# Down projections of two feed-forward layers: 16 of the 22 hidden chunks by seven-product (Strassen) blocks in two phases

## The chip, the cores and the metric

The kernel runs on one core of a Trainium2 chip. The metric is the device time of one execution in microseconds, the median over several runs. Beside it stands one execution recorded by the hardware profiler, from which all durations are taken.

## The reference

A residual stream h of 1024 positions by 1024 features passes through two layers; each adds a mixer and then a gated feed-forward network, with an RMS norm in front of each, and a last norm ends the program. The change touches only the feed-forward network:

```python
def conv_glu_ffn(x, w_up, conv_w, conv_b, w_down):
    h = causal_depthwise_conv(x @ w_up, conv_w, conv_b)
    gate, val = jnp.split(h, 2, axis=-1)
    return (jax.nn.silu(gate) * val) @ w_down
...
h = h + conv_glu_ffn(rmsnorm(h, ffn_norm[layer]), ffn_up[layer], ffn_conv_w[layer],
                     ffn_conv_b[layer], ffn_down[layer])
```

The hidden width is 2816, which is 22 chunks of 128; gate and value each have 22 chunks. Everything is float32.

## The kernel before

Activations lie transposed, features on the 128 partitions and the 1024 tokens along the row. TensorE multiplies in fp32r, which keeps fewer bits, so every operand is split into a high part (a cast on ScalarE, line 338) and a low part (the difference, on VectorE, line 339), and each product is three matmuls: high x high, high x low, low x high. A matmul has a 128 x 128 weight block and 512 tokens, half of a row. `Weights` (lines 72 to 140) streams weight blocks in the order of a plan: a load on the SP queue into one of two raw buffers `wst` (three while `W.more` is set), then the split (line 116) into a ring of `wh`/`wl` pairs.

The feed-forward network `ffn(ly, norms)` has two stages.

*Up.* For each chunk f of 22, gate and value come from one block of seven products of 12 matmuls each instead of eight (lines 772 to 818, matmuls in line 637): the weights and the tokens are first combined by additions. Beside the products of chunk f run the convolution, silu and product of chunk f-1 (class `Tail`): two activations for the last tap (lines 653, 654), four taps on VectorE (659), silu on ScalarE (667), the product (673), and a store of the 128 x 1024 result to DRAM, tensor `hid` (674). The operands of the up stage lie in AH and AL (8 slots of 1024 tokens) and TH and TL (three sets of 4 x 512).

*Down.* The hidden chunks come back from DRAM, `stage(f, slot)` (lines 731 to 734): a load into a `t4` buffer (four of them) and a split into a slot of AH/AL or TH/TL. They are taken in groups of 8, 6 and 8 chunks in layer 0 and 8, 6, 4 and 4 in layer 1. For each group, each of the 8 output chunks oc and each token half, `down` (831) accumulates all chunks of the group in one of four PSUM banks (839), and VectorE adds the bank to the residual hT (841), which was loaded from DRAM, `hdr`, at the start of the stage (828, 829). The buffers of the up stage and hT share memory, so that load waits until the last chunk's result is stored. In layer 0 the last group runs one token half after the other, with its weights fetched once for each half, and the next norm is woven into it (952 to 964); while that goes on, the pool engine makes the low parts of the next weights (961). In layer 1 the last four chunks are multiplied the other way round, tokens as weights, and end in the output (`finish`).

A scheduler of the compiler lays out the instructions of each engine, by the order of the program and by when it reckons an instruction ready; each engine then works its list in order, and so does the SP queue, which issues nearly all transfers.

Of the kernel before, what the change touches and what calls it, by code (L numbers as in the profile page):

```python
# [37 lines left out]
GROUPS = {0: [(0, 8), (8, 6), (14, 8)], 1: [(0, 8), (8, 6), (14, 4), (18, 4)]}  # L38
# [33 lines left out]
class Weights:  # L72
# [3 lines left out]
    def __init__(self, nc, pool, plan):  # L76
        self.nc, self.pool, self.plan = nc, pool, plan
        self.eng = nc.vector
        self.more = None
        self.raw, self.ready = [], {}  # L80
        self.n_dma = self.n_conv = self.n_get = self.n_take = 0
        self.n_ring = 0

    def _dma(self, n=None):
        n = n or NWST + (self.more is not None)
        while self.n_dma < min(self.n_conv + n, len(self.plan)):
# [10 lines left out]
    def pair(self):  # L97
# [3 lines left out]
        if self.more is not None and n % 5 > 2:  # L101
            return [self.more.tile([P, DC, P], F32R, tag=t, bufs=2, name=f"{t}x{n}")
                    for t in ("wh2", "wl2")]
# [40 lines left out]
def trunk(ctx: ExitStack, tc: tile.TileContext, x, mix0_norm, mix0_w_in, lru_conv_w, lru_conv_b,  # L144
# [12 lines left out]
    plan = []  # L157
# [8 lines left out]
    def plan_ffn(ly):  # L166
# [6 lines left out]
        def dn(h, f0, n):  # L173
            for oc in range(DC):
                plan.append((f"{ly}d{h}{f0}{oc}",
# [3 lines left out]
        for f0, n in GROUPS[ly]:  # L179
# [6 lines left out]
            else:  # L186
                dn("0", f0, n)
                dn("1", f0, n)
# [91 lines left out]

    def open_h(name):
        st["pool"] = tc.tile_pool(name=f"h_{name}", bufs=1, side="right")
        p = st["pool"].__enter__()
        st["hT"] = p.tile([P, DC, T], F32, name=f"hT_{name}")

    def close_h():
        st["pool"].__exit__(None, None, None)
        st["hT"] = None
# [284 lines left out]
    hid = [dram.tile([P, NF, T], F32, name=f"hid{i}") for i in range(2)]  # L573

    def ffn(ly, norms):

# [16 lines left out]
        w2 = [None]  # L593

# [47 lines left out]
        def t4x(name):  # L642
            return w2[0].tile([P, T], F32, tag="t4x", bufs=2, name=name)


        class Tail:
            def __init__(self, f, g, v):
                self.f, self.g, self.v = f, g, v

            def ident(self):  # L650
                f, new = self.f, t4x if w2[0] is not None else t4
                self.cg, self.cv = new(f"cg{ly}{f}"), new(f"cv{ly}{f}")
# [19 lines left out]
            def end(self):  # L672
                dve.tensor_tensor(self.cv, self.cv, self.cg, op=ALU.mult)
                nc.sync.dma_start(hid[ly][:, self.f], self.cv)
# [8 lines left out]
            def whole(self):  # L683
                self.ident()
                self.rest()

# [19 lines left out]
        def tokens(p1):  # L706
# [14 lines left out]
            w2_cm = tc.tile_pool(name=f"w2{ly}", bufs=1)  # L721
            W.more = w2[0] = w2_cm.__enter__()
# [8 lines left out]
        def stage(f, slot):  # L731
            r = t4(f"hr{ly}{f}")
            nc.sync.dma_start(r, hid[ly][:, f])
            split(*slots[slot], r)

# [35 lines left out]

        for f in range(2, NF):
            w, nxt = ws.pop(f), f + 1 if f + 1 < NF else None
# [27 lines left out]
            act.copy(u3, X)  # L801
# [3 lines left out]
            else:  # L805
                for c in range(4):
                    stage(c, c)
# [3 lines left out]
            if nxt:  # L811
                prep_b(nxt)
            prod(X, w["c"], 4, "4", False)
# [5 lines left out]
        W.ahead(2)  # L819
        for c in range(4, 8):  # L820
            stage(c, c)
        prev.rest()
        W.more = w2[0] = None
        w2_cm.__exit__(None, None, None)
# [3 lines left out]
        for c in range(DC):  # L828
            nc.sync.dma_start(hT[:, c], hdr[:, c])

        def down(h, tag, f0, a, oc):
            wh, wl = W.get(f"{ly}d{tag}{f0}{oc}")
# [10 lines left out]
        def finish(f0, a):  # L843
# [81 lines left out]
            for tt in range(DC - 1):  # L925
# [5 lines left out]
                if tt + 2 < DC:  # L931
# [5 lines left out]

        plans = {0: (slots[0:8], [(8 + i, 8 + i) for i in range(6)]),
                 8: (slots[8:14], [(14 + i, i) for i in range(8)]),
                 14: (slots[0:8] if ly == 0 else slots[0:4], []),  # L940
                 18: (slots[4:8], [])}
        for f0, n in GROUPS[ly]:
            a, todo = plans[f0]
            if f0 + n < NF:
                for oc in range(DC):
                    down(None, "x", f0, a, oc)
                    for f, c in todo[oc:oc + 1]:
                        stage(f, c)
            elif ly:
                finish(f0, a)  # L950
            else:
                new = [Norm(0, gcols[after], f"nf{ly}"), Norm(1, gcols[after], f"nf{ly}")]
                rsqrt_set()
                for h in range(2):
                    for oc in range(DC):
                        down(h, str(h), f0, a, oc)
                        if after.startswith("mix"):
                            nc.sync.dma_start(hdr[:, oc, HALF[h]], hT[:, oc, HALF[h]])
                        if h == 1 and oc == 0:
                            new[0].rstd()  # L960
                            W.eng = pool
# [3 lines left out]
        W.eng = dve  # L965
# [618 lines left out]
```

## Time and profile before

| what | value |
|---|---|
| runs, us | 2176.86 median of 3 (2176.27 to 2177.23) |
| the profiled execution, us | 2175.29 |
| its span, first to last instruction, us | 2173.6 |
| granted TensorE clock, mean | 0.998 |
| first down stage, us from the start | 778 to about 1022, 1056 matmuls in line 839 |
| second down stage, up to the last four chunks | 1916 to about 2115, 864 matmuls in line 839 |
| data moved | 212.19 MB, 98 GB/s on the mean |

The page of a profile gives busy time by engine, the span in 40 slices, the DMA queues, the chain of work that ended last and the costliest groups of instructions. A group names the line, engine, operation and tiles, then busy time, mean length of one and the idle time in front of them with what ended it. Matmuls overlap: the length of one in a group is not the pitch at which they follow each other. Other views give the busy time of the engines in any stretch, the timeline of one engine, and who waited for whom.

### The profile page before, as it was taken

Reading aid. Unit: us, or ns where it says so; the run is one execution under the profiler, and the core shown is the slowest. Engines: PE = TensorE matmul, PEld = TensorE weight load, DVE = VectorE, ACT = ScalarE, POOL = GpSimd, SP = SyncE. Lnnn points to the kernel's source line nnn. Section 1 sums busy time; section 2 is a strip of 40 time slices with the busy share of each in tenths; the row PEclk is TensorE's granted clock in tenths of the full one; section 3 lists DMA queues with packets and bytes.
Section 4 is the critical chain, followed back from the end, with each engine's and each line's share of the span. In section 5 each row is a group of like instructions: output and inputs, shape, how many; then the busy total and the mean of one; then the engine's idle time right before and its main releaser. Section 6 shows DMA issues by size and latency. Waiting matters only on the chain. (4 is left out here: it accounts for less than half of the span.)

```text
span 2173.6 us, 25612 instructions
## 1 busy us (share of the span) xinstructions
PE 2138.9 (98%) x9865; PEld 1757.0 (81%) x9865; DVE 1455.4 (67%) x2075; ACT 1016.3 (47%) x1405; POOL 95.4 (4%) x128
## 2 busy tenths in 40 slices
PE   8999999999999999999999999899999999999998
PEld 7888888788888878887778887788778888888887
DVE  6655657987777763347576667868987777763334
ACT  5433544655555541124556565744655555541113
POOL 0000001000000000004111111010000000000000
PEclk9999999999999999999999999999999999999999
DMA  5111342232222282234221211442232222382112
GB/s 149 53 49 49 112 149 88 87 107 84 73 77 88 92 285 73 84 121 131 73 66 52 74 56 54 159 153 81 88 107 87 84 71 78 97 292 94 56 54 78
DMA packets 263329, 212.19 MB, mean 98 GB/s; under 512 B 8336, under 2 KB 233424, under 8 KB 263208
## 3 DMA queue, kind: packets, MB, share of 16 engines
q1 hardware_dynamic: 262872, 210.08, 31.0%
q8 instruction: 77, 1.26, 0.2%
q0 software_dynamic: 192, 0.30, 0.1%
q14 instruction: 44, 0.36, 0.1%
q10 hardware_dynamic: 144, 0.20, 0.0%
HBM read 165.15 MB, written 43.29 MB: 96 GB/s over the span
## 5 line engine op out<-in xcount | busy, mean ns | idle before, releaser
L116 ACT CAST wh<-wst 128x1024 fp32r<-128x1024 f32 (+2 forms) x134 | 134.1, 1001 | 491.7 <-PE dp L839 274.6
L841 DVE TENSOR_TENSOR hT_f<-dp,hT_f 128x512 f32<-128x512 f32 x96 | 65.9, 690 | 225.2 <-PE dp L839 224.0
L116 DVE TENSOR_TENSOR wl<-wst,wh 128x1024 fp32r<-128x1024 f32 (+2 forms) x127 | 146.8, 1156 | 96.7 <-ACT wh L116 96.7
L839 PE MATMUL dp<-AH,wh 128*128 128x512 f32 x432 | 168.1, 391 | 1.4 <-DVE hT_f L841 1.3
L839 PE MATMUL dp<-AL,wh 128*128 128x512 f32 x432 | 167.9, 389 | 0.3 <-DVE AL L339 0.3
L839 PE MATMUL dp<-AH,wl 128*128 128x512 f32 x432 | 167.9, 389 | 0.0
L637 PE MATMUL X<-TH,wh 128*128 128x512 f32 x312 | 121.9, 391 | 1.9 <-ACT u L757 0.9
L637 PE MATMUL X<-TH,wl 128*128 128x512 f32 x312 | 121.7, 390 | 0.3 <-DVE wl L339 0.3
L637 PE MATMUL X<-TL,wh 128*128 128x512 f32 x312 | 121.4, 389 | 0.0
L659 DVE SCALAR_TENSOR_TENSOR cg<-g,par_c,cg 128x1023 f32<-128x1023 f32 x88 | 112.7, 1280 | 2.0 <-ACT cg L653 1.9
L659 DVE SCALAR_TENSOR_TENSOR cv<-v,par_c,cv 128x1023 f32<-128x1023 f32 x88 | 112.5, 1278 | 1.2 <-ACT cv L654 1.1
L338 ACT CAST wh<-wst 128x1024 fp32r<-128x1024 f32 x78 | 80.6, 1053 | 61.4 <-PE YZ L637 38.3
L339 DVE TENSOR_TENSOR wl<-wst,wh 128x1024 fp32r<-128x1024 f32 x78 | 95.1, 1223 | 6.6 <-ACT wh L338 6.6
L839 PEld LDWEIGHTS dp<-AH,wh 128*128 128x128 f32 x432 | 81.1, 188 | 19.4 <-DVE hT_f L841 1.7
L839 PEld LDWEIGHTS dp<-AL,wh 128*128 128x128 f32 x432 | 81.1, 188 | 17.7 <-DVE AL L339 0.7
L839 PEld LDWEIGHTS dp<-AH,wl 128*128 128x128 f32 x432 | 81.1, 188 | 16.8
L345 PE MATMUL op<-AH,wh 128*128 128x512 f32 x192 | 76.3, 397 | 0.6 <-ACT hT_o L520 0.6
L637 PE MATMUL X<-TH,wh2x 128*128 128x512 f32 x192 | 74.8, 390 | 0.7 <-ACT u L791 0.7
L637 PE MATMUL YZ<-AH,wh 128*128 128x512 f32 x192 | 74.9, 390 | 0.0
L345 PE MATMUL op<-AH,wl 128*128 128x512 f32 x192 | 74.8, 390 | 0.0
L345 PE MATMUL op<-AL,wh 128*128 128x512 f32 x192 | 74.8, 389 | 0.0
L637 PE MATMUL YZ<-AL,wh 128*128 128x512 f32 x192 | 74.7, 389 | 0.0
(487 smaller groups left out, 5854.6 us busy)
## 6 DMA issues: line engine op xcount, KB each, us to landing
wst<-in_ffn_up_dram SPq DMA_DIRECT2D x88, 512.0 KB
hid<-cv SPq DMA_DIRECT2D x44, 512.0 KB
hr<-hid SPq DMA_DIRECT2D x44, 512.0 KB
wst<-in_mix_w_in_dram SPq DMA_DIRECT2D x40, 512.0 KB
wst<-in_ffn_down_dram SPq DMA_DIRECT2D x35, 512.0 KB
wst<-in_mix_w_out_dram SPq DMA_DIRECT2D x32, 512.0 KB
hdr<-hT_o SPq DMA_DIRECT2D x32, 256.0 KB
hT_f<-hdr SPq DMA_DIRECT2D x16, 512.0 KB
```

The costliest lines, as they stand in the source:

```text
L116: did = self.nc.scalar.copy(wh[:, :k, :m], w[:, :k, :m]), self.eng.tensor_tensor(wl[:, :k, :m], w[:, :k, :m], wh[:, :k, :m].bitcast(F32), ...
L338: return (act.copy(h, src), (eng or dve).tensor_tensor(l, src, h.bitcast(F32), op=ALU.subtract))
L339: (eng or dve).tensor_tensor(l, src, h.bitcast(F32), op=ALU.subtract))
L345: last_mm = pe.matmul(ps, a[:, k], b[:, k, s], start=(k == 0 and i == 0), stop=(k == DC - 1 and i == 2))
L637: last = pe.matmul(ps, a[:, k0 + k], b[:, k], start=(first and k == 0 and i == 0), stop=(k == 3 and i == 2), skip_group_check=True)
L659: dve.scalar_tensor_tensor(dst[:, dl:], src[:, :T - dl], taps[j](c), dst[:, dl:], op0=ALU.mult, op1=ALU.add)
L839: pe.matmul(ps, p_[:, k], q_[:, s], start=(k == 0 and i == 0), stop=(k == n - 1 and i == 2))
L841: dve.tensor_tensor(hT[:, oc, s], ps, hT[:, oc, s], op=ALU.add)
```

## The change

Chunks 0 to 15 are multiplied in two groups of eight by blocks of seven products (Winograd's form of Strassen's method). The even and the odd chunks of a group are the two halves of the inner dimension, the two token halves are the columns, and two pairs of output chunks the rows; so a block covers 8 chunks, 4 output chunks and all tokens. A product is 2 output chunks (e = 0, 1) x 4 chunks x 3 matmuls of 512 tokens. The seven products are parted by the operands they read. Form A has "11", "2", "3", "4", whose token operands lie in AH and AL, form B has "1", "21", "22" in TH and TL. One form for one set of four output chunks is a `Quad`; the order is A, A, B, B for the first group, then the same for the second. Running sums stay in PSUM: all products of form A go into the same two banks, and after each one VectorE adds the bank to the part of hT that it completes (56 such additions per layer; the first quad's eight are copies on ScalarE that start hT).

Token sums: the up stage computes them beside its products (`Tail.sums`: one half-size subtraction after an even chunk, three after an odd one) and stores seven operands per pair of chunks in a new DRAM tensor `hids`. `bring` loads half an operand and splits it; the lists `beside` say which of them follow each half product. Weight sums: `Quad.x11`, `s2`, `s3`, `s4` compute them on VectorE; two of them (`s`, `s2`) go to DRAM in form A and come back in form B. `prep(n + 2)` runs two products ahead, and loads for the next quad are issued at fixed steps of it.

Chunks 16 to 21 stay plain: six in layer 0, with weights split once and kept in TH and TL for both token halves; two and then four in layer 1. The pool engine no longer makes low parts of weights at the end of layer 0. hT is two tiles of four output chunks; rows 4 to 7 are loaded from `hdr` at the start of the stage, rows 0 to 3 are added during the second form-A phase (`residual_in`). The ring of weight pairs shrinks from five to four in the up stage, and the buffers of the convolution are one `cg` and two `cv`, by even and odd chunk.

```diff
-GROUPS = {0: [(0, 8), (8, 6), (14, 8)], 1: [(0, 8), (8, 6), (14, 4), (18, 4)]}
+EIGHTS = (0, 8)
+PLAIN = {0: [(16, 6)], 1: [(16, 2), (18, 4)]}
+OPS = {"11": 0, "2": 1, "4": 2, "3": 3, "21": 4, "22": 5, "1": 6}
 HALF = (slice(0, H), slice(H, T))
...
-                dn("1", f0, n)
...
+        for i in (1, 0):
+            cm = tc.tile_pool(name=f"h{i}_{name}", bufs=1, side="right")
+            st["pool"].append(cm)
+            tiles.insert(0, cm.__enter__().tile([P, 4, T], F32, name=f"hT{i}_{name}"))
+        st["hT"] = Halves(tiles)
...
+                self.cg, self.cv = (w2[1].tile([P, T], F32, tag=t, name=f"{t[:2]}{ly}{f}")
+                                    for t in ("cg", f"cv{f % 2}"))
...
+                f, to, k = self.f, hids[ly][self.f // 8 % 2], self.f % 8 // 2
+                if f >= PLAIN[ly][0][0]:
+                    nc.sync.dma_start(hid[ly][:, f], self.cv)
+                elif f % 2:
+                    nc.sync.dma_start(to[:, 4:6, k],
+                                      self.cv.rearrange("p (s t) -> p s t", t=H))
+                else:
+                    nc.sync.dma_start(to[:, OPS["11"], k], self.cv[:, HALF[0]])
+            def sums(self):
+                f, to, k = self.f, hids[ly][self.f // 8 % 2], self.f % 8 // 2
+                if f >= PLAIN[ly][0][0]:
+                    return
+                b1, b2 = (self.cv[:, s] for s in HALF)
+                if f % 2 == 0:
+                    t1 = w2[0].tile([P, H], F32, tag="t1", name=f"t1{ly}{f}")
+                    dve.tensor_tensor(t1, b2, b1, op=ALU.subtract)
+                    nc.sync.dma_start(to[:, OPS["1"], k], t1)
+                    Tail.even = self.cv, t1
+                else:
+                    ev, t1 = Tail.even
+                    Tail.even = None
+                    e1, e2 = (ev[:, s] for s in HALF)
+                    dve.tensor_tensor(t1, b2, t1, op=ALU.subtract)
+                    dve.tensor_tensor(e2, b2, e2, op=ALU.subtract)
+                    dve.tensor_tensor(e1, b1, t1, op=ALU.subtract)
+                    nc.sync.dma_start(to[:, OPS["2"], k], t1)
+                    nc.sync.dma_start(to[:, 2:4, k], ev.rearrange("p (s t) -> p s t", t=H))
...
+        def bring(g, y, j):
+            ks = slice(2 * j, 2 * j + 2)
+            r = t4(f"br{ly}{g}{y}{j}").rearrange("p (k t) -> p k t", k=2)
+            nc.sync.dma_start(r, hids[ly][g][:, OPS[y], ks])
+            split(*(t[:, ks] for t in B[y]), r)
...
+            def load(self, i):
+                def wst(n, src):
+                    t = self.raw[n] = wpool.tile([P, DC, P], F32, tag="wst", bufs=NWST,
+                                                 name=f"{n}{self.name}")
+                    nc.sync.dma_start(t if n == "s1" else two(t), src)
+                def small(n, src):
+                    t = self.raw[n] = [t2(f"{n}{e}{self.name}").rearrange("p (k m) -> p k m", k=4)
+                                       for e in range(2)]
+                    for e in range(2):
+                        nc.sync.dma_start(t[e], src(e))
+                if self.form == "A":
+                    if i == 0:
+                        wst("x11", self.block(0, self.oc, 2))
+                    else:
+                        wst("x21", self.block(0, self.oc + 2, 2))
+                        small("x22", lambda e: self.block(1, self.oc + 2 + e, 1))
+                elif i == 0:
+                    wst("s1", self.sum[0].rearrange("p e k m -> p (e k) m"))
+                else:
+                    wst("x12", self.block(1, self.oc, 2))
+                    small("s2", lambda e: self.sum[1][:, e])
...
+            def x11(self):
+                split(*self.pair("11"), self.raw["x11"])
+                s = self.raw["s"] = [t2(f"s{e}{self.name}").rearrange("p (k m) -> p k m", k=4)
+                                     for e in range(2)]
+                for e in range(2):
+                    dve.tensor_tensor(s[e], one(self.raw["x21"], e), self.raw["x22"][e],
+                                      op=ALU.add)
+                    nc.sync.dma_start(self.sum[0][:, e], s[e])
+            def s2(self):
+                s = self.raw.pop("s")
+                for e in range(2):
+                    dve.tensor_tensor(s[e], s[e], one(self.raw["x11"], e), op=ALU.subtract)
+                    nc.sync.dma_start(self.sum[1][:, e], s[e])
+                self.split2("2", s)
+            def s3(self):
+                t, a = self.raw.pop("x21"), self.raw.pop("x11")
+                dve.tensor_tensor(t, a, t, op=ALU.subtract)
+                split(*self.pair("3"), t)
+            def x22(self):
+                self.split2("4", self.raw.pop("x22"))
+            def s1(self):
+                split(*self.pair("1"), self.raw.pop("s1"))
+            def x12(self):
+                split(*self.pair("21"), self.raw["x12"])
+            def s4(self):
+                t, a = self.raw.pop("s2"), self.raw.pop("x12")
+                for e in range(2):
+                    dve.tensor_tensor(t[e], one(a, e), t[e], op=ALU.subtract)
+                self.split2("22", t)
...
+            def prod(self, n, e):
+                bank = (n == "21", e)
+                first = n in ("11", "1", "21")
+                if first:
+                    self.ps[bank] = psml(f"dq{self.name}{n}{e}")
+                ps = self.ps[bank]
+                (xh, xl), (yh, yl) = self.w[n], B[n]
+                for k in range(4):
+                    for i, (a, b) in enumerate(((xh, yh), (xh, yl), (xl, yh))):
+                        pe.matmul(ps, a[:, 4 * e + k if n == "1" else 2 * k + e], b[:, k],
+                                  start=(first and k == 0 and i == 0),
+                                  stop=(k == 3 and i == 2), skip_group_check=True)
+                row, s = {"11": (0, A0), "2": (0, A1), "3": (1, A1), "4": (1, A0),
+                          "1": (1, A1), "21": (0, A0), "22": (0, A1)}[n]
+                at = st["hT"][:, self.oc + 2 * row + e, s]
+                if self.form == "A" and self.g == 0 and self.oc == 0:
+                    act.copy(at, ps)
+                else:
+                    dve.tensor_tensor(at, ps, at, op=ALU.add)
+                if n in ("4", "21", "22"):
+                    del self.ps[bank]
+                if e:
+                    del self.w[n]
...
+        quads = [Quad(g, oc, form) for g in range(2) for form in "AB" for oc in (0, 4)]
+        steps_ = [(q, i) for q in quads for i in range(len(q.preps))]
+        def prep(n):
+            q, i = steps_[n]
+            q.preps[i]()
+            nxt = quads.index(q) + 1
+            if nxt < len(quads):
+                if q.form == "A":
+                    loads = {2: (0, 1)}.get(i, ())
+                else:
+                    loads = {0: (0,), 2: (1,)}.get(i, ())
+                for j in loads:
+                    quads[nxt].load(j)
...
+        n_kept = PLAIN[0][0][1]
+        kept = [[t.rearrange("p a b t -> p (a b t)").rearrange(
+            "p (o k m) -> p o k m", o=DC, m=P)[:, oc] for t in (TH, TL)] for oc in range(DC)]
+        def kept_in(oc):
+            split(*kept[oc], W.take(f"{ly}d0{PLAIN[0][0][0]}{oc}")[:, :n_kept])
+            W.done()
+        def lead_in(i):
+            if ly == 0:
+                kept_in(i)
+            else:
+                W.ahead(i + 1)
+        def residual_in(c):
+            r = t4(f"hd{ly}{c}")
+            nc.sync.dma_start(r, hdr[:, c])
+            dve.tensor_tensor(hT[:, c], hT[:, c], r, op=ALU.add)
+        beside = {(0, "A"): first_[6:] + brings(0, ("1", "21", "22")),
+                  (0, "B"): brings(1, ("11", "2", "3", "4")),
+                  (1, "A"): [x for c, b in enumerate(brings(1, ("1", "21", "22")))
+                             for x in [b] + ([lambda c=c: residual_in(c)] if c < 4 else [])],
+                  (1, "B"): [lambda i=i: stage(PLAIN[ly][0][0] + i, i) for i in range(6)]}
+        for n, (q, i) in enumerate(steps_):
+            todo = beside[q.g, q.form]
+            for e in range(2):
+                q.prod(q.prods[i], e)
+                if e == 0 and n + 2 < len(steps_):
+                    prep(n + 2)
+                if todo:
+                    todo.pop(0)()
+            if n == len(steps_) - 2:
+                W.limit = None
+                W._dma()
+                lead_in(0)
+            elif n == len(steps_) - 1:
+                lead_in(1)
...
+        for f0, n in PLAIN[ly]:
+            a = slots[f0 - PLAIN[ly][0][0]:][:n]
...
-                        down(h, str(h), f0, a, oc)
+                        if not h and oc + 2 < DC:
+                            kept_in(oc + 2)
+                        down(h, kept[oc], f0, a, oc)
                         if after.startswith("mix"):
                             nc.sync.dma_start(hdr[:, oc, HALF[h]], hT[:, oc, HALF[h]])
                         if h == 1 and oc == 0:
                             new[0].rstd()
-                            W.eng = pool
```

127 lines of the change are left out of this document (89 added, 38 removed).

## The prediction

> **What bounds the kernel now.** I read the page first, then the busy time by stage, the chain of waits, the groups of the two stages that change, and last the waits and the timeline around the change of stage.
>
> ```profile
> span 2173.6 us, 25612 instructions
> ...
> PE 2138.9 (98%) x9865; PEld 1757.0 (81%) x9865; DVE 1455.4 (67%) x2075; ACT 1016.3 (47%) x1405; POOL 95.4 (4%) x128
> ```
>
> Busy time by stage: the up and the down stage of layer 0, then those of layer 1; the columns are start:end, length, then each engine's busy time (instructions), granted clock, DMA share and GB/s.
>
> ```profile
> 389.00:778.00 389.00, 387.94 (x1707) 319.70 (x1706) 311.60 (x339) 209.97 (x253) 0.00 (x0) 1.00 0.31 95
> 778.00:1022.00 244.00, 242.35 (x1064) 199.16 (x1064) 116.01 (x122) 68.47 (x78) 24.49 (x11) 1.00 0.41 134
> 1512.00:1916.00 404.00, 401.68 (x1762) 329.54 (x1761) 325.37 (x351) 221.32 (x264) 0.00 (x0) 1.00 0.30 93
> 1916.00:2115.00 199.00, 198.18 (x877) 163.47 (x876) 81.97 (x96) 42.23 (x46) 0.00 (x0) 1.00 0.35 117
> ```
>
> TensorE is full in both stages. VectorE has 116 of 244 us of work in the first down stage and 82 of 199 in the second, but 80% in the up stages. So matmuls taken out of a down stage shorten it one for one, as long as VectorE, ScalarE and the DMA queues keep up with what replaces them.
>
> The chain of waits gives the pitch of the matmuls (start, length, work):
>
> ```profile
> 1862.58 2.72 PE YZ L637 x12
> ...
> 1925.86 188.45 PE dp L839 x830
> ```
>
> 188.45 / 830 = 0.227 us, and 2.72 / 12 is the same. The groups of the first down stage give one matmul as 391 ns (busy, mean | idle before, releaser):
>
> ```profile
> L839 PE MATMUL dp<-AH,wh 128*128 128x512 f32 x194 | 75.1, 391 | 1.4 <-DVE hT_f L841 1.3
> ```
>
> That is a pipelined length, not a price; I reckon with 0.227.
>
> **The matmuls removed.** Eight chunks, four output chunks and both token halves cost 8 x 4 x 3 x 2 = 192 matmuls now. A pair of quads makes them with 7 products x 2 output chunks x 4 k x 3 = 168. There are two groups of eight and two sets of four output chunks in each layer: 4 x 24 = 96 less per layer, 192 in all, and the page should count 9,865 - 192 = 9,673. 192 x 0.227 = **-43.5 us**. Sixteen chunks still cost 672 matmuls, 152.4 us, in each layer; the plain rest is unchanged in kind.
>
> **VectorE in the new products.** The prices, from the groups of the first down stage and, for an operand of half size, of the second up stage:
>
> ```profile
> L841 DVE TENSOR_TENSOR hT_f<-dp,hT_f 128x512 f32<-128x512 f32 x40 | 27.5, 690 | 106.7 <-PE dp L839 105.5 <-DMA hT_f<-hdr 1.2
> ...
> L339 DVE TENSOR_TENSOR AL<-hr,AH 128x1024 fp32r<-128x1024 f32 x12 | 14.2, 1221 | 2.5 <-ACT AH L338 2.4
> L338 ACT CAST AH<-hr 128x1024 fp32r<-128x1024 f32 x12 | 12.3, 1050 | 10.4 <-PE dp L839 5.5 <-DMA hr<-hid 4.9
> ...
> L659 DVE SCALAR_TENSOR_TENSOR cg<-g,par_c,cg 128x1023 f32<-128x1023 f32 x1 | 1.3, 1284 | 1.4 <-ACT cg L653 1.4
> ```
>
> ```profile
> L339 DVE TENSOR_TENSOR dl<-s,dh 128x512 fp32r<-128x512 f32 x15 | 10.3, 685 | 1.9 <-ACT dh L338 1.9
> ```
>
> A half-size operation is 0.69 us, a full one 1.22. A form-A quad has 8 evictions and, for its weights, 3 full and 8 half operations: 5.5 + 9.2 = 14.7 us in 8 x 2.72 = 21.8 us of products. A form-B quad has 6 evictions, 2 full and 4 half: 9.3 us in 16.3. Four of each make 96.0 us per layer; ScalarE takes the first quad's 8 evictions (-5.5). The lists beside the products hold 8 + 8 + 10 + 6 = 32 entries of 1.22 us, 39.0. With the last chunk's four taps and its product (4 x 1.28 + 1.22 = 6.3) that is 135.8 us of 152.4, 89%, where the old stage had 116 of 244.
>
> What stalls is finer. Every half product ends in an eviction. In form A the next one into the same bank comes 2.72 us later, so the eviction has 2.72 - 0.69 = 2.0 us to spare (in form B a bank rests one product longer). Queued ahead of it on VectorE are a share of a weight preparation and an entry. In form A a half product with an entry is 0.69 + 9.2/8 + 1.22 = 3.06 us of VectorE against 2.72; in form B 0.69 + 5.2/6 + 1.22 = 2.78. Eighteen of the entries lie in form A, fourteen in B: 18 x 0.34 + 14 x 0.06 = 7.0 us per layer if nothing is made up, and nothing if the 24 halves without entry (at most 1.84 us of work each) make it up. Bounds 0 and 7.0; I take **+3 per layer**, nearer the lower end, since VectorE has run full in this kernel without TensorE losing a matmul:
>
> ```profile
> 380.00:399.00 19.00, 18.77 (x83) 15.25 (x82) 19.00 (x20) 13.82 (x15) 0.00 (x0) 1.00 0.19 55
> 399.00:418.00 19.00, 18.16 (x77) 13.95 (x77) 18.09 (x20) 12.31 (x15) 0.00 (x0) 1.00 0.26 84
> 418.00:437.00 19.00, 19.00 (x85) 15.59 (x85) 19.00 (x22) 10.95 (x15) 0.00 (x0) 1.00 0.33 110
> ```
>
> In the third row VectorE is busy all 19 us and 85 matmuls pass (19 / 0.227 = 84); in the second it costs 7 of them, 1.6 us.
>
> **The handover from up to down.** There are 21.8 us, the first quad, before the second quad's operands are due. VectorE needs by then: the tail 6.3, operands "3" and "4" 4.9, the weights s2, s3, x22 of this quad 6.6 and x11 of the next 2.6, together 20.4; s2 of the next, 2.8, is due one product later. Popped among these are the six entries of form B's operands, 7.3, which are not due before 43.5 us. Behind everything else they cost nothing; ahead of everything, 20.4 + 2.8 + 7.3 = 30.5, 8.7 late. Two of them stand ahead of x11 and four ahead of s2, so with each at its place x11 is late by 20.4 + 2.4 - 21.8 = 1.0, and what is still queued is some 2 us longer than its time: I take 2.7 (0 to 8.7). The residual is the other part. From the instructions of the down products' line, then VectorE's and SP's timelines:
>
> ```profile
> L839 PE MATMUL dp<-AH,wh x432: 387/389/799, 778.3 to 2113.5; 128*128 128x512 f32 x144
> ```
>
> ```profile
> 790.02 1.22 DVE L673 TENSOR_TENSOR cv<-cv,cg 128x1024 f32<-128x1024 f32 x1
> ...
> 801.80 2.60 DVE L841 TENSOR_TENSOR hT_f<-dp,hT_f 128x512 f32<-128x512 f32 x4 [1.16 <-DMA hT_f<-hdr]
> ```
>
> ```profile
> 791.27 0.32 SPq L674 DMA_DIRECT2D hid<-cv  x1
> ...
> 795.92 5.54 SPq L829 DMA_DIRECT2D hT_f<-hdr  x8
> ```
>
> The last chunk's product ends at 791.2, 13 us after the first down matmul (778.3); SP then waits until 795.9 for its store to land, and only 5.9 us later the first eviction finds its residual, 23.5 us after the start. Now eight evictions wait for that; then the first four rows of hT need no load, and the first eviction that adds to a loaded row ends its product at 21.8 + 2.7 = 24.5 us. It just fits: 0, or the 1.3 us that TensorE waits for it today, which I take. Together **+4 per layer** (0 to 10.0). On the SP queue the other loads wait behind this one. Beside it lie some 12 MB in the first 43.5 us (operands 5, residual 2, last chunk 0.5, weights 3, sums 1.5), 276 GB/s; the same place has carried more:
>
> ```profile
> 797.00:816.00 19.00, 17.73 (x78) 14.36 (x77) 8.92 (x11) 5.16 (x5) 0.00 (x0) 1.00 0.92 335
> ```
>
> **The up stage.** Of a pair of chunks the sums add four half operations, 2.8 us, 1.4 per chunk, against 19.04 us of products (7 x 2.72) in which VectorE works 14.6:
>
> ```profile
> 475.00:494.00 19.00, 19.00 (x85) 15.75 (x84) 14.63 (x17) 9.88 (x13) 0.00 (x0) 1.00 0.27 83
> ```
>
> In this steady state they lie in VectorE's idle 4.4 us. In the first three chunks it has none (the rows above): 0 to 3 x 1.4 = 4.2; I take **+1 per layer**. Stores grow from 1 to 1.75 MB per pair on queues at 83 GB/s: nothing. With one buffer of cv for the even chunks, ScalarE's next write waits for the store of the sums; without slack that would be a few tenths in eight chunks, hidden behind the products now in front of its next copy.
>
> **Into the next layer.** The pool engine no longer makes the low parts of the next weights; VectorE does, behind the norm: 0 to 4 x 1.22 = 4.9. The pool's work slows VectorE today, so some comes back:
>
> ```profile
> 1001.08 2.70 DVE L309 TENSOR_TENSOR ss_nf<-ss_nf,sq_nf 128x512 f32<-128x512 f32 x1
> ...
> 1022.84 0.69 DVE L309 TENSOR_TENSOR ss_nf<-ss_nf,sq_nf 128x512 f32<-128x512 f32 x1
> ```
>
> I take **+1.5** once. The eight weight loads that fall away were hidden and bring nothing.
>
> Sum: -43.5 + 2 x (3 + 4 + 1) + 1.5 = **-26.0**. The profiled execution took 2175.3 us (span 2173.6), so 2149.3; the median shown is 1.6 above that execution, so **2151**.
>
> **The rivals.**
> *All of it is covered.* VectorE catches up everywhere and the residual wait goes as well: -43.5 - 2 x 1.3 = -46.1, 2131. For it speaks the third row above, against it 89% over a whole stage.
> *VectorE sets the pace.* Both vector terms at their upper ends: -43.5 + 2 x (10.0 + 7.0 + 1) + 1.5 = -6.0, 2171. With every other bound at its end too (4.2 and 4.9) it is 2 x 21.2 + 4.9 - 43.5 = +3.8, about no change.
> *Late operands make it slower.* An entry's low part stands in VectorE's queue until its load has landed, and the eviction stands behind it. Today the casts of such loads wait:
>
> ```profile
> ACT AH L338 <- DMA hr<-hid: 15.6, 16, 2.4
> ...
> ACT TH L338 <- DMA hr<-hid: 8.1, 10, 2.1
> ```
>
> 23.7 us in 26 waits, 0.91 each, harmless with four banks of 5.4 us ahead. If all 64 entries lost that on TensorE's path: 58 us, -43.5 + 58 + 2 x 2.3 + 1.5 = +21, 2198. It decides from (43.5 - 6) / 64 = 0.59 us per entry. Against it: the 2.0 us to spare, and that these waits lie where queues run at 273 to 335 GB/s, while the later phases, counted as above, move 8, 9.5 and 5.5 MB in 32.7, 43.5 and 32.7 us, 245, 218 and 168 GB/s.
> *The clock drops.* At the start of the kernel TensorE idles, and its clock is cut:
>
> ```profile
> 10.00:20.00 10.00, 5.70 (x36) 5.33 (x37) 9.18 (x19) 7.06 (x14) 0.00 (x0) 0.83 0.72 185
> 20.00:30.00 10.00, 10.00 (x73) 10.00 (x73) 6.48 (x17) 6.67 (x14) 0.00 (x0) 0.83 0.90 297
> ```
>
> 4.3 us idle and 0.17 x 20 = 3.4 us lost to the clock, 7.7. One such stop at each handover in place of my 4 gives -26.0 + 2 x 3.7 = -18.6, 2158. The Trainium skill, TensorE: Matmul & The Clock Gate, section on HAM oscillation, speaks against the change here: cycling through PSUM banks between groups of matmuls leaves TensorE idle often enough for its clock to fall back to half. By that rule most of the products could run at half rate. The trace does not bear it out where it has the same pattern: the up stages copy a bank between every two products and keep a clock of 1.00 in the rows by stage. So only the single long stop keeps a chance.
>
> **How the numbers follow.** Forecast 0.62, all covered 0.12, VectorE's pace 0.12, late operands 0.07, clock 0.05, every bound at its end 0.02. The range 2136 to 2172 holds the forecast's own spread, the clock case, VectorE's pace and half of the covered case; the slow cases and the rest of the best are left out. Two measurements of this kernel can be told apart from about 0.2%, 4.4 us: faster 0.89, same 0.04, slower 0.07.
>
> **What would show it.** 9,673 matmuls at a pitch of 0.227; 217.6 us of matmuls in the first down stage, 174.1 in the second before the last four chunks. Right: TensorE's waits there name VectorE's evictions, a few us per layer, most within 45 us of the handover and at the start of the second form-A phase. Wrong: waits on evictions of over 15 us per layer, VectorE's own waits naming loads of operands or weights, a clock under 0.99 in a down stage, or lost matmuls in the up stages beyond their first four chunks.

## The result, and the profile after

The median went from 2176.57 us (four runs, 2173.28 to 2177.23) to 2156.8 us (four runs, 2156.19 to 2158.41). That is 19.8 us less; the ratio is 0.9913, with an interval of 0.9896 to 0.993. The profiled execution of the changed kernel has a span of 2154.6 us, against 2173.6 before: 19.0 less. The forecast was 25 to 26 less, so the change is faster as forecast, and gives about 6 us less than forecast.

The head of the page of the changed kernel, to be held against the same two lines of before:

```profile
span 2154.6 us, 25867 instructions
...
PE 2102.5 (98%) x9673; PEld 1720.3 (80%) x9673; DVE 1599.4 (74%) x2306; ACT 1062.9 (49%) x1485; POOL 74.7 (3%) x121
```

There are 9,673 matmuls, 192 fewer, and VectorE has 144 us more work. Where the 19 us lie is read from the first matmul of each stage; an up stage begins with the plain products of its first chunk, in both layers:

| stretch, us | before | after | difference |
|---|---|---|---|
| start to first up matmul of layer 0 | 352.9 | 353.9 | +1.0 |
| up, layer 0 | 425.4 | 428.0 | +2.6 |
| down, layer 0 | 242.9 | 231.5 | -11.4 |
| mixer of layer 1 | 467.6 | 466.5 | -1.1 |
| up, layer 1 | 428.0 | 427.2 | -0.9 |
| down, layer 1, without the last four chunks | 197.3 | 188.2 | -9.1 |
| end | 59.4 | 59.4 | 0.0 |

The two down stages should have lost 21.8 us each (96 matmuls of 0.227). They lost 11.4 and 9.1. Busy time of the changed kernel by stretch; columns as in the prediction. The first row is the up stage of layer 0; the next three are its down stage, cut into the handover, the later products and the plain chunks; the last two are the handover and the later products of layer 1:

```profile
354.00:782.00 428.00, 425.59 (x1864) 348.23 (x1863) 361.18 (x409) 225.17 (x274) 0.00 (x0) 1.00 0.31 98
782.00:852.00 70.00, 63.07 (x266) 50.06 (x265) 57.96 (x66) 38.97 (x49) 0.00 (x0) 0.98 0.90 304
852.00:947.00 95.00, 93.21 (x409) 75.98 (x408) 73.68 (x94) 33.20 (x40) 0.94 (x1) 1.00 0.56 185
947.00:1013.00 66.00, 66.00 (x291) 54.28 (x290) 34.47 (x48) 20.25 (x29) 3.86 (x3) 1.00 0.36 112
...
1907.00:1978.00 71.00, 64.36 (x265) 51.04 (x264) 57.16 (x65) 38.94 (x48) 0.00 (x0) 0.95 0.90 301
1978.00:2073.00 95.00, 93.20 (x408) 75.96 (x407) 72.54 (x93) 31.16 (x38) 0.00 (x0) 1.00 0.53 175
```

The handover is the two form-A quads and the first form-B quad of the first group: 264 matmuls, 59.9 us at 0.227. It takes 70.0 us in layer 0 and 71.1 in layer 1, with DMA queues 90% busy and a clock below 1.00. The later products lose 2.7 and 2.8 us, and the plain chunks nothing. So most of the missing gain lies in the handover. TensorE's waits in the down stage of layer 0 (tile and line of the waiting matmul, what it waited for, us in total, times, longest):

```profile
PE dq004A L922 <- ACT wh L361: 3.6, 2, 3.2
PE dq000A L922 <- DVE wl L362: 1.7, 2, 0.9
PE dq010A L922 <- DVE hT_f L931: 1.4, 2, 1.2
PE dq000A L922 <- ACT hT_f L929: 0.9, 1, 0.9
PE dq000A L922 <- ACT wh L361: 0.8, 1, 0.8
PE dq014A L922 <- DVE hT_f L931: 0.4, 1, 0.4
```

The names are those of the quads (dq, layer, group, first output chunk, form): dq004A is the second form-A quad (layer 0, group 0, output chunks 4 to 7). Its 3.2 us, the longest stop of the stage, is a wait for a weight, not for an eviction. Layer 1 has the same stop, again of 3.2 us, in dq104A. Which weight it is, VectorE's timeline tells (x11004A is the next quad's first weight block, TL the low part of an entry of form B):

```profile
801.81 1.22 DVE L362 TENSOR_TENSOR wl<-x11004A,wh 128x1024 fp32r<-128x1024 f32 x1
...
804.49 0.69 DVE L881 TENSOR_TENSOR s0004A<-x21004A,x220004A 128x512 f32<-128x512 f32 x1 [0.32 <-DVE AL L362]
...
806.96 1.22 DVE L362 TENSOR_TENSOR TL<-br,TH 128x1024 fp32r<-128x1024 f32 x1
812.19 0.69 DVE L931 TENSOR_TENSOR hT_f<-dq004A,hT_f 128x512 f32<-128x512 f32 x1 [4.01 <-PE dq004A L922]
814.45 0.69 DVE L931 TENSOR_TENSOR hT_f<-dq004A,hT_f 128x512 f32<-128x512 f32 x1 [1.58 <-PE dq004A L922]
815.10 1.22 DVE L362 TENSOR_TENSOR TL<-br,TH 128x1024 fp32r<-128x1024 f32 x1
816.25 0.69 DVE L888 TENSOR_TENSOR s0004A<-s0004A,x11004A 128x512 f32<-128x512 f32 x1
```

The weight sum s is made at 804.49. The next sum, s2 = s - x11 (line 888), takes nothing from the operations between, yet it comes at 816.25, and VectorE idles for 4.01 and 1.58 us meanwhile. Line 888 writes its result over s, and s is being stored to DRAM: by the program the operation must not begin before that store has read s. In VectorE's list it stands behind two evictions of its own quad, which wait for their products, and behind an entry; it starts right after them. So this timeline alone does not show whether the store still held it at 816.25 or only that place in the list, which the scheduler gave it. The SP queue at the same place:

```profile
803.01 1.74 SPq L1058 DMA_DIRECT2D hT_f<-hdr  x4
804.85 1.29 SPq L808 DMA_DIRECT2D br<-hids  x1
806.18 0.79 SPq L883 DMA_DIRECT2D sum<-s0004A  x1
```

The store is issued at 806.18, right behind 2 MB of residual (rows 4 to 7 of hT). What the stop does to TensorE, first in its timeline and then in stretches of 2 us:

```profile
814.03 0.39 PE L922 MATMUL dq004A<-AH,wl 128*128 128x512 f32 x1
817.64 0.80 PE L922 MATMUL dq004A<-AH,wh 128*128 128x512 f32 x1 [3.22 <-ACT wh L361]
818.23 0.63 PE L922 MATMUL dq004A<-AL,wh 128*128 128x512 f32 x1
818.66 0.63 PE L922 MATMUL dq004A<-AH,wl 128*128 128x512 f32 x1
819.08 0.63 PE L922 MATMUL dq004A<-AH,wh 128*128 128x512 f32 x1
```

```profile
812.00:814.00 2.00, 2.00 (x10) 1.68 (x9) 0.69 (x1) 0.00 (x0) 0.00 (x0) 1.00 1.04 411
...
818.00:820.00 2.00, 2.00 (x6) 1.48 (x6) 1.75 (x3) 2.00 (x4) 0.00 (x0) 0.50 1.10 315
...
822.00:824.00 2.00, 2.00 (x11) 1.63 (x10) 2.00 (x3) 1.46 (x3) 0.00 (x0) 1.00 0.53 208
```

From 814.03 to 817.64 are 3.61 us where 0.23 would do: 3.4 us. Then the matmuls follow each other every 0.42 to 0.43 us in place of 0.227, because the granted clock is 0.50. From 817.64 to 820.72 this costs another 1.5 us. So the one late weight costs about 4.9 us, half of the 10.1 that the handover loses. The other half, five stops of 0.3 to 0.9 us, lies in the first quad. Layer 1 has a second drop of the clock there, after a stop of 1.58 us for a copy on ScalarE; hence the 0.95.

### The profile page after: what moved, and what is told of

The parts are those of the page before. It is cut to its first block, busy times and chain, and to the rows that moved or that the text cites. A ratio compares the mean times of both kernels' runs of the same rounds, so it can differ in the third digit from the quotient of the medians.

```text
span 2154.6 us, 25867 instructions
## 1 busy us (share of the span) xinstructions
PE 2102.5 (98%) x9673; PEld 1720.3 (80%) x9673; DVE 1599.4 (74%) x2306; ACT 1062.9 (49%) x1485; POOL 74.7 (3%) x121
## 5 line engine op out<-in xcount | busy, mean ns | idle before, releaser
L121 ACT CAST wh<-wst 128x1024 fp32r<-128x1024 f32 (+1 forms) x87 | 86.3, 992 | 224.6 <-PE op L368 45.1
L121 DVE TENSOR_TENSOR wl<-wst,wh 128x1024 fp32r<-128x1024 f32 (+1 forms) x87 | 100.1, 1151 | 98.4 <-ACT wh L121 98.2
L668 PE MATMUL X<-TH,wh 128*128 128x512 f32 x384 | 150.0, 391 | 1.8 <-ACT u L1012 1.4
L690 DVE SCALAR_TENSOR_TENSOR cv<-v,par_c,cv 128x1023 f32<-128x1023 f32 (+1 forms) x88 | 112.5, 1278 | 0.1
L668 PE MATMUL YZ<-AH,wl 128*128 128x512 f32 x240 | 93.4, 389 | 0.0
L668 PEld LDWEIGHTS X<-TH,wh 128*128 128x128 f32 x384 | 72.1, 188 | 18.6 <-ACT u L1012 2.6
L668 PEld LDWEIGHTS X<-TH,wl 128*128 128x128 f32 x384 | 72.1, 188 | 16.6 <-DVE wl L362 1.6
L668 PEld LDWEIGHTS X<-TL,wh 128*128 128x128 f32 x384 | 72.1, 188 | 14.9
L368 PE MATMUL op<-AH,wh 128*128 128x512 f32 x192 | 76.3, 397 | 0.6 <-ACT hT_o L543 0.6
L684 ACT ACTIVATE cg<-g,par_c 128x1024 f32<-128x1024 f32 x44 | 54.8, 1246 | 28.8 <-DVE g L1034 24.2
L1557 ACT ACTIVATE P<-P,sm 128x128 f32<-128x128 f32 (+3 forms) x64 | 49.7, 777 | 29.9 <-DVE sm L1554 29.6
```

The costliest lines, as they stand in the source:

```text
L121: did = self.nc.scalar.copy(wh[:, :k, :m], w[:, :k, :m]), self.eng.tensor_tensor(wl[:, :k, :m], w[:, :k, :m], wh[:, :k, :m].bitcast(F32), ...
L368: last_mm = pe.matmul(ps, a[:, k], b[:, k, s], start=(k == 0 and i == 0), stop=(k == DC - 1 and i == 2))
L668: last = pe.matmul(ps, a[:, k0 + k], b[:, k], start=(first and k == 0 and i == 0), stop=(k == 3 and i == 2), skip_group_check=True)
L684: act.activation(self.cg, self.g, AF.Identity, scale=taps[2](f), bias=bias(f))
L690: dve.scalar_tensor_tensor(dst[:, dl:], src[:, :T - dl], taps[j](c), dst[:, dl:], op0=ALU.mult, op1=ALU.add)
L1557: act.activation(Pt[:, :n], Pt[:, :n], AF.Exp, bias=low, scale=-1.0, accum_out=sm[:, 6:7])
```

## The experiments

Two theories were set against each other. *The store wait*: s2 overwrites a tile that is still being stored, so its own tile takes the stop away. *The crowded handover*: the queues and VectorE carry too much in these 60 us, so entries and the residual must leave. Beside them stood the token sums in the up stage. All ratios are against the kernel before, run on the same chip; "handover" is the stretch of 264 matmuls in layer 0 and in layer 1.

| run | median, us | ratio (interval) | handover, us |
|---|---|---|---|
| the change | 2156.8 | 0.9913 (0.9896 to 0.993) | 70.0, 71.1 |
| e1_own | 2140.95 | 0.9847 (0.9833 to 0.986) | 65.0, 64.2 |
| e2_late | 2148.77 | 0.9879 (0.9866 to 0.9893) | 69.2, 65.1 |
| e3_res | 2148.35 | 0.9878 (0.9863 to 0.9893) | 67.2, 66.9 |
| e4_nosum | 2166.43 | 0.9965 (0.9952 to 0.9977) | 78.0, 76.3 |
| e5_own4 | 2147.19 | 0.9874 (0.9857 to 0.989) | 67.7, 65.6 |
| e6_pad | 2156.29 | 0.9915 (0.99 to 0.993) | 70.1, 71.9 |
| e7_own_late | 2145.29 | 0.9863 (0.9847 to 0.988) | 65.7, 67.4 |
| e8_own_late_res | 2144.21 | 0.9862 (0.9847 to 0.9876) | 65.3, 67.8 |

**e1_own: a tile of its own for s2**, in every form-A quad but the first of each layer.

```diff
-                    dve.tensor_tensor(s[e], s[e], one(self.raw["x11"], e), op=ALU.subtract)
-                    nc.sync.dma_start(self.sum[1][:, e], s[e])
-                self.split2("2", s)
+                    dve.tensor_tensor(d[e], s[e], one(self.raw["x11"], e), op=ALU.subtract)
+                    nc.sync.dma_start(self.sum[1][:, e], d[e])
+                self.split2("2", d)
```

> In three of four form-A quads of a layer the second weight sum goes to a tile of its own instead of overwriting the first one, so it need not wait until the first one's store has been read. Theory 'store wait' (the late weights of the second quad come from that overwrite): the 3.2 us wait of TensorE in the second quad and the lower clock behind it go, about -4 us per layer, 2149 us in all. Theory 'crowded handover' (the entries for form B stand ahead of these weights, on full DMA queues): less than 1 us per layer, 2155 to 2157.

Measured: 0.9847, the lowest time of all, 34.0 us under the median of the kernel before on the same chip (2174.95); against the change the two ratios give 0.9847 / 0.9913 = 0.9933, some 14 us. VectorE's timeline of this run:

```profile
803.64 0.69 DVE L883 TENSOR_TENSOR s0004A<-x21004A,x220004A 128x512 f32<-128x512 f32 x1 [0.64 <-DVE AL L362]
804.25 0.69 DVE L883 TENSOR_TENSOR s1004A<-x21004A,x221004A 128x512 f32<-128x512 f32 x1
804.85 0.69 DVE L895 TENSOR_TENSOR d0004A<-s0004A,x11004A 128x512 f32<-128x512 f32 x1
```

The difference now follows the sums at once, 24.1 us after the first down matmul (780.8) in place of 34.3 (781.9), and ahead of the evictions. TensorE's wait for that quad's weights falls from 3.6 to 0.3 us, and its clock stays up although the queues are as full as before:

```profile
PE dq004A L929 <- ACT wh L361: 0.3, 1, 0.3
```

```profile
810.00:820.00 10.00, 10.00 (x46) 8.28 (x45) 8.16 (x10) 5.09 (x7) 0.00 (x0) 1.00 1.02 390
```

That the overwrite is the cause is shown: without it 5.0 and 6.9 us of the two handovers are gone, more than was expected of it. The edit takes away the wait for the store and, with it, the late place in VectorE's list; it does not part the two. DMA queues at a share of 1.02 do not by themselves stop TensorE.

**e2_late: six empty places ahead of the entries of form B.**

```diff
-        beside = {(0, "A"): first_[6:] + brings(0, ("1", "21", "22")),
+        beside = {(0, "A"): first_[6:] + [lambda: None] * 6 + brings(0, ("1", "21", "22")),
```

> The six loads and splits of form B's operands in the first group move from the first quad to the second; nothing else is changed. 'Crowded handover': the DMA share in the first 20 us falls below 0.9 and the 3.2 us wait in the second quad goes, -4 to -5 us per layer, 2147 to 2149 us. 'Store wait': the wait stays, at most 1 us per layer, 2155.

Measured: 0.9879, between the change and e1_own. That is the time that 'crowded handover' had forecast. Layer 1 gains 6.0 us in the handover, layer 0 only 0.7. In layer 1 VectorE waits only 0.57 us for the store, TensorE 0.4 at most for the weight, no stop is long, and the clock stays at 1.00; in layer 0 it falls twice. What is left in layer 0 now carries its own name, in VectorE's timeline and the SP queue of this run:

```profile
814.79 0.69 DVE L888 TENSOR_TENSOR s0004A<-s0004A,x11004A 128x512 f32<-128x512 f32 x1 [1.86 <-DMA sum<-s0004A]
```

```profile
803.23 1.74 SPq L1058 DMA_DIRECT2D hT_f<-hdr  x4
805.26 0.32 SPq L883 DMA_DIRECT2D sum<-s0004A  x1
```

VectorE waits for the store of s: 9.5 us from the issue of 256 KB, behind the residual, until line 888 may write. Only one eviction now stands between s and s2, at 812.24, and line 888 waits 1.86 us beyond it: this is the store itself. The entries had stood ahead of s2 as well, and without them s2 is not earlier than the store allows.

**e3_res: no residual load at the handover.** All quads of the first group start hT by copies on ScalarE, and all eight rows are added in the second form-A phase.

```diff
-        for c in range(4, DC):
-            nc.sync.dma_start(hT[:, c], hdr[:, c])
...
-                if self.form == "A" and self.g == 0 and self.oc == 0:
+                if self.form == "A" and self.g == 0:
```

> No residual is loaded at the handover: the second quad's eight evictions become copies on ScalarE too, and all eight rows of the residual are added in the second form-A phase (four entries more there). 'Crowded handover': 2 MB less in the first 30 us, -2 to -4 us per layer there, +0.5 in the second form-A phase, 2150 to 2154 us. 'Store wait': no change at the handover, 2157 to 2158.

Measured: 0.9878, the same as e2_late; 'store wait' had forecast no gain. The residual no longer stands ahead of the store (SP queue, then VectorE):

```profile
803.37 0.32 SPq L883 DMA_DIRECT2D sum<-s0004A  x1
```

```profile
807.29 0.68 DVE L888 TENSOR_TENSOR s0004A<-s0004A,x11004A 128x512 f32<-128x512 f32 x1
```

3.9 us from the issue to line 888, in place of 9.5 or 10.1, and line 888 no longer waits. The second quad's evictions have also left VectorE's list, so the run does not part these two. By the times written down before, e2 and e3 fit 'crowded handover' and e1 fits 'store wait'. The timelines join them: the tile of s made VectorE wait for a transfer, and what stood in front of that transfer set how long. In exchange the four rows more that are added later cost time there: in layer 1 the third form-A quad takes 27.4 us, against 24.0 in the change.

**e5_own4, e7_own_late and e8_own_late_res: own tiles for every quad, the first one too, and then with the two edits above.** The first quad's difference goes to a free buffer of the convolution. e7 adds the empty places of e2, e8 also drops the residual load, with rows 4 to 7 added in the second form-B phase.

```diff
+                if self.g == 0 and self.oc == 0:
+                    t = w2[1].tile([P, T], F32, tag="cv0", name=f"d{self.name}")
+                    d = [t[:, h].rearrange("p (k m) -> p k m", k=4) for h in HALF]
```

> As the run with a tile of its own for the second weight sum, now in the first quad of each layer too (in a buffer of the convolution that is free then). 'Store wait': the 0.6 to 0.8 us that VectorE waits there for the first sum's store goes, and TensorE's waits of 0.9 us on the weights of product '2' shrink: -1 to -2 us per layer, 2137 to 2139 us. 'Crowded handover': that wait is covered by others, no change, 2140 to 2141.

> Own tiles in all four form-A quads, and form B's operands of the first group moved to the second quad. If store wait and crowding add: 2132 to 2135 us, handover near 61 to 62 us per layer (59.9 is its matmuls alone). If the crowding only mattered through the late weight sums: no gain over own tiles alone, 2137 to 2140.

> The same, and no residual is loaded at the handover: the second quad's evictions are copies too, rows 4 to 7 are added beside the last form-B products, where half the steps have no entry. 'Crowded handover': another -1 to -2 us per layer, 2130 to 2133 us. If the DMA load no longer matters once the weights are early: within 1 us of the run before it.

Measured: 0.9874, 0.9863 and 0.9862, in place of the 2130 to 2141 us that were expected; none is ahead of e1_own, though the intervals touch or overlap. Removing the first quad's store wait gained nothing and seems to have cost some 6 us. TensorE's timeline and clock in e5_own4:

```profile
788.75 0.50 PE L930 MATMUL dq000A<-AH,wh 128*128 128x512 f32 x1 [1.54 <-ACT hT_f L937]
...
797.82 0.80 PE L930 MATMUL dq000A<-AH,wh 128*128 128x512 f32 x1 [1.74 <-ACT hT_f L937]
```

```profile
798.00:800.00 2.00, 2.00 (x5) 1.61 (x6) 2.00 (x2) 1.77 (x2) 0.00 (x0) 0.50 0.86 304
```

With the weights ready early, the copies of the first products come behind casts of weights and of entries in ScalarE's order; TensorE stops for 1.5 and 1.7 us on them, and the clock halves. And the two edits that were worth 7 us each on the change (0.9879 and 0.9878 against 0.9913) add nothing measurable to e5_own4, whose interval overlaps those of e7 and e8. This fits that what they had gained was mainly an earlier s2. It is not shown: in all three runs TensorE waits 2.8 to 3.5 us per layer for copies of the first quad, against 1.0 and 0.3 in e1_own, and the two edits were not run on e1_own.

**e4_nosum and e6_pad: the token subtractions left out**, to price them in the up stage; e6 keeps the tile that e4 no longer needs.

```diff
-                    t1 = w2[0].tile([P, H], F32, tag="t1", name=f"t1{ly}{f}")
-                    dve.tensor_tensor(t1, b2, b1, op=ALU.subtract)
+                    t1 = b2
...
-                    dve.tensor_tensor(t1, b2, t1, op=ALU.subtract)
-                    dve.tensor_tensor(e2, b2, e2, op=ALU.subtract)
-                    dve.tensor_tensor(e1, b1, t1, op=ALU.subtract)
```

> Left out: the token subtractions of the up stage (the plain halves are stored in their place, so all transfers remain and the result is not the reference's). If they cost what the up stage of layer 0 grew by, that stage falls by 2.6 us and the whole to 2154; if they lie in idle time and the 2.6 us come from elsewhere (the changed order of the list, the smaller ring of weights), the stage stays within 0.5 us, 2156 to 2157.

> Left out as before: the token subtractions (plain halves are stored, so the result is not the reference's); but the small tile that held one of the sums keeps its place in memory. If the waits of 15 us for hT's first copy in the earlier run came from hT's memory moving onto the convolution's buffers, they are gone, the handover takes 70 us again as in the changed kernel, and the whole shows the price of the subtractions: 2153 to 2156 us. If they came from leaving out the work itself, they stay and it takes 2166.

Measured: with less work e4 is slower than the change, 0.9965, where 2154 to 2157 us were expected. The up stage of layer 0 takes 427.5 us against 428.0; the loss is in the handovers, 78.0 and 76.3. One stop carries it, in TensorE's waits and in ScalarE's timeline of e4:

```profile
PE dq000A L917 <- ACT hT_f L924: 15.7, 1, 15.7
```

```profile
801.13 1.07 ACT L924 COPY hT_f<-dq000A 128x512 f32<-128x512 f32 x2 [0.34 <-DMA hid<-cv]
```

The first copies into hT wait until the last chunk's result is stored. The tile that fell away had stood in front of the convolution's buffers; without it hT came to lie, as far as the wait tells, over one that was still in use. e6 keeps it, leaves the subtractions out all the same, and is back at 0.9915. So the layout was the cause of e4, and the token sums cost nothing that can be measured: 0.9915 against 0.9913, and 427.6 against 428.0 us in the up stage of layer 0.

## Why the prediction was right, and where it missed

**Matmuls removed: -43.5, right.** 9,673 matmuls, as counted. The stretches without stops keep the pitch: the second form-B quad of the first group, 72 matmuls, takes 16.3 us in both layers.

**VectorE in the new products: +3 per layer, right.** The later products lose 2.7 and 2.8 us, most of it at the start of the second form-A phase, as expected. The page's VectorE total rose by 144 us, and TensorE's waits on its evictions are 1.8 us per layer. But part of the size is luck: nearly half of it is one late operand, not work queued on VectorE; ScalarE's and VectorE's timelines of the changed kernel:

```profile
874.60 1.05 ACT L361 CAST TH<-br 128x1024 fp32r<-128x1024 f32 x1 [5.34 <-DMA br<-hids]
```

```profile
875.69 1.22 DVE L362 TENSOR_TENSOR TL<-br,TH 128x1024 fp32r<-128x1024 f32 x1 [2.63 <-ACT TH L361]
876.83 0.68 DVE L931 TENSOR_TENSOR hT_f<-dq010A,hT_f 128x512 f32<-128x512 f32 x1
```

This is the rival of the late operands: a load in front of an eviction in VectorE's order. It exists, and is the longest wait of dq010A above, 1.2 us, once in each layer; not 0.59 us in each of 64 entries, from which it would have decided.

**Handover from up to down: +4 per layer, the term that was mis-sized.** Measured were 10.1 and 11.2 us. The old down stages had 2.4 and 1.2 us of stops of their own (their length less their matmuls at 0.227, and less 0.8 for the norm in layer 0), so the term is +7.7 and +10.0: 9.7 us more than the two fours. With the other terms (-0.5 in the later products, -0.3 in the up stages, -2.6 into the next layer, +1.0 at the start) that makes about 7, and the miss was 7.0 of the span. The bound of 10.0 just held. The step that failed is the sum behind "x11 is late by 20.4 + 2.4 - 21.8 = 1.0" and "s2 of the next, 2.8, is due one product later": it gave each weight operation its duration and its place in VectorE's queue, and no dependence on a transfer. x11 was in time: its low part is begun at 801.81, 19.9 us after the first down matmul. s2 was not: by the same sum, with four entries ahead of it, it is done after 20.4 + 2.8 + 4.9 = 28.1 us and due after 27.2; line 888 began after 34.3. The store of s, which line 888 must wait for before it can write over s, stood in the diff, and no term priced it. It took 9.5 us in e2_late, measured up to line 888. The residual wait, the other part of the term, did not come: no wait of TensorE or VectorE names the load of hT. As far as e2_late and e3_res show, the load cost time as 2 MB in front of that store instead.

The price of that stop had a second part. *The clock drops* was a rival at 0.05, and it happened inside the forecast: 3.2 us of waiting and some 1.5 us lost at half clock behind the late weight, in each handover. It was not a separate case but a surcharge on a stop. Its other half, the rule of the Trainium skill (TensorE: Matmul & The Clock Gate, A second HAM failure mode) that cycling through PSUM banks makes the clock swing between half and full rate, did not come true here either: the later products alternate between two banks after every 12 matmuls and keep 1.00 for 95 us.

**Up stage: +1 per layer; the sum right, the reason not.** +2.6 and -0.9 make 1.7. But e6_pad has no token subtractions and still needs 427.6 us in layer 0, so they are not what the 2.6 is. TensorE's waits there grew from 1.1 to 2.4 us; the weight ring of four pairs and the single buffers of the convolution were not tested, and the cause stays open. That the two layers nearly add up to the forecast is luck. The +1.0 ahead of it, before any changed instruction, lies within what the nine profiles of changed kernels show for that stretch, 352.2 to 354.2 us.

**Into the next layer: +1.5, wrong in sign, small.** The stretch became 1.1 us shorter. The operation that took 2.71 us beside the pool engine's work takes 0.69 in the changed kernel, in the same place:

```profile
1015.02 0.69 DVE L332 TENSOR_TENSOR ss_nf<-ss_nf,sq_nf 128x512 f32<-128x512 f32 x1
```

No run put the pool's work back alone, so that this is the reason is read from the trace and not shown.

**What would show it.** "TensorE's waits there name VectorE's evictions" was right only for the later products. In the handover they name casts of weights and copies on ScalarE. Of the signs of a wrong forecast two appeared: the clock was 0.98 in the down stage of layer 1 (0.99 in layer 0), and VectorE waited once per layer, 2.5 and 2.4 us, for the load of a weight block, x12010B and x12110B, without a stop of TensorE.

## What to carry to other kernels

An operation that overwrites a tile must wait for every transfer that still reads it; where a store of that tile stands in the same few lines, price the store behind what is queued in front of it, or give the result a tile of its own. Here that tile, four kilobytes per partition for both halves, was worth some 14 us, beside the 19.8 that the whole change had brought. When an edit shortens one engine's list and the kernel gets slower, look at where tiles came to lie and how the order of the other engines moved before believing anything of the edit itself.

## What the hardware showed

The clock falls in one step to 0.50, and up to the last matmul of these runs it stays there for 3.41 us or a whole multiple of it: from 817.21 to 820.63 in the changed kernel, from 797.04 to 803.86 in e5_own4. No single long stop is needed for it. In e2_late two stops of 0.94 and 0.93 us within 3 us were enough (TensorE's timeline):

```profile
788.15 0.50 PE L922 MATMUL dq000A<-AH,wh 128*128 128x512 f32 x1 [0.94 <-ACT wh L361]
...
789.82 0.53 PE L922 MATMUL dq000A<-AH,wl 128*128 128x512 f32 x1 [0.93 <-DVE wl L362]
```

In the changed kernel the same pair of stops, 0.80 and 0.89 us, left the clock at 1.00; in e1_own, 0.63 and 0.90 did. Within a run all drops begin a whole number of times 3.41 us apart. Cut into pieces at these edges, the two runs differ in how long TensorE worked in the piece with the stops, 1.54 and 1.75 us (e2_late, then the changed kernel; the second row of each is the next piece):

```profile
786.73:790.14 3.41, 1.54 (x6) 0.65 (x5) 3.41 (x5) 3.41 (x7) 0.00 (x0) 1.00 0.76 246
790.14:793.56 3.42, 3.42 (x10) 2.67 (x8) 3.42 (x4) 2.33 (x3) 0.00 (x0) 0.50 0.96 236
```

```profile
786.49:789.90 3.41, 1.75 (x7) 0.82 (x5) 3.05 (x5) 3.41 (x6) 0.00 (x0) 1.00 0.73 229
789.90:793.31 3.41, 3.38 (x15) 2.80 (x16) 3.41 (x4) 3.41 (x6) 0.00 (x0) 1.00 0.95 217
```

In the down stages of these runs every full-clock piece in which TensorE worked for less than 1.55 us was followed by a drop, and none in which it worked for more than 1.85 was; between the two both occur. So where the stops fall among these pieces seems to decide as well as their length. The Trainium skill (TensorE: Matmul & The Clock Gate, HAM oscillation) warns of idle gaps of more than about 3.4 us. The 3.2 us of the handover, 3.6 from matmul to matmul, agree with that roughly; the drop after two stops of 0.9 does not. A few short stops close together are therefore to be counted with a surcharge, by estimate up to 1.7 us for each piece of 3.41 at half clock; 1.5 were measured behind the late weight.

A store of 256 KB had cleared its tile at the latest 3.9 us after its issue when the 2 MB of residual did not stand in front of it (e3_res), and 9.5 us after when they did (e2_late), both at a DMA share near 0.95.
